# HGRN scores in 32-wide column tiles: small levels as gathered 32x32 blocks, large levels without masks

## The chip, the cores and the metric

The kernel runs on one core of a Trainium2 chip. The metric is device time in microseconds (us) of one execution, the median of several runs; lower is better. A core has TensorE (in the profile PE for matmuls and PEld for the loads of their weights), VectorE (DVE), ScalarE (ACT), GpSimd (POOL) and SyncE (SP, which here issues the weight DMAs).

## The reference

Four post-norm residual layers over 256 tokens of width 1024, each with a token mixer and a SwiGLU feed-forward part. Layers 0 and 3 mix with HGRN2, layer 1 with mLSTM, layer 2 with S5. Only HGRN matters here, with 8 heads of 128 channels:

```python
    log_f = jnp.logaddexp(jnp.log(lb), jnp.log1p(-lb) + jax.nn.log_sigmoid(f))
    k = (1.0 - lb) * jax.nn.sigmoid(-f)
    q = jax.nn.silu(q.astype(jnp.float32))
...
        b = jnp.cumsum(lfb, axis=2)
        diff = b[:, :, :, None, :] - b[:, :, None, :, :]
        decay = jnp.exp(jnp.where(mask[:, :, None], diff, -jnp.inf))
        att = jnp.einsum('bhtd,bhsd,bhtsd->bhts', qb, kb, decay)
        o = jnp.einsum('bhts,bhse->bhte', att, vb) + jnp.einsum('bhtd,bhde->bhte', qb * jnp.exp(b), s_prev)
```

A score of query t and key s is a sum over channels of q times k times the product of the forget gates between s and t, channel by channel. The decay depends on the channel, so it cannot be taken out of the product of q and k.

## The kernel before, in words

All matmuls on weights split their operands into two parts of type F32R (`hi` and `lo`) and take three matmuls (`mm3`, L140 to L142; a wide form at L170 and L173). The weights come in by DMA on SP's queue in 1 MB pieces; ACT copies `hi` (L123), DVE subtracts to get `lo` (L124). A planner keeps the pieces one ahead of their use. The order of instructions on each engine is set when the kernel is built; every engine then works through its list in order, and waits on semaphores.

`hgrn` works on pairs of heads, four pairs to a layer. `hgrn_scores` takes a pair with q and k as tiles of 128 channels by 512 columns: four parts of 128 tokens, in the order (half 0, head 0), (half 0, head 1), (half 1, head 0), (half 1, head 1). It builds the 128x128 score matrices `att` of the four parts, keys in the rows (partitions) and queries in the columns, in a tree. The diagonal comes first: one matmul for each part (L583), multiplied by the identity on DVE (L584). Then, for block sizes m = 1, 2, 4, ... 64, keys of one block of m tokens meet queries of its sibling block: the upper one of each 2m tokens in the first half of the tokens, the lower one in the second half, which is held in reverse.

At a level, ACT gathers the keys side by side into `kk` (L592, 128x256), two matmuls of 128x128 give all their scores with the queries (L594), and DVE's COPY_PREDICATED with a mask from `msk` (L598) puts the wanted ones into `att`. At m = 64 two ACT copies (L609) do this in place of the mask. DVE then multiplies the gate products into k and q for the next level and joins neighbouring products (all through `mul`, L572). A last pair of matmuls (L616) gives the scores between the two halves. `scores` runs two pairs side by side, level by level, and places other work of the layer between the levels: projections of the next queries, of v and of the gate, and `heads_out`, which multiplies the scores with v (L489, L491).

These matmuls read F32 as it is, without a split. Each F32 matmul stands in the trace as two PE records with a weight load each; below, one record is called a pass.

The S5 layer has two other kinds of matmuls that use part of TensorE's columns and that the prediction reads: L1002 and L1004 write 32 partitions from 32 columns of weights, always the same 32; L1090 writes partitions 0 to 63 and 64 to 127 in turn from 64 columns of weights:

```python
                    for f in range(4):
                        for x in range(3):
                            for e in range(2):
                                outputs(py[64 * e : 64 * e + 64, col(f)], b - 1 + e, f, x)
```

Of the kernel before, what the change touches and what calls it, by code (L numbers as in the profile page):

```python
# [9 lines left out]
F32 = mybir.dt.float32  # L10
# [4 lines left out]
ALU = mybir.AluOpType  # L15
AX = mybir.AxisListType

P = 128
# [9 lines left out]
HEAD_EPS = 1e-6  # L28
MASKED = (1, 2, 4, 8, 16, 32)
BIG = 1e30  # L30
# [4 lines left out]
class Trunk:  # L35
# [395 lines left out]
    def hgrn(self, j, gb, lb=None):  # L431

        nc, tc = self.nc, self.tc
        nw = self.const.tile([P, 1], F32, name=f"hnw{j}")
        nc.gpsimd.dma_start(nw, self.a["hg_nw"][j])
        with tc.tile_pool(name=self.uid("hg"), bufs=1, reuse_waits="tile") as hp, \
                tc.tile_pool(name=self.uid("hw"), bufs=2, reuse_waits="tile") as wp:
            msk = hp.tile([P, len(MASKED), 256], F32, name=self.uid("msk"))
            nc.gpsimd.dma_start(msk, self.a["c_lvl"])
# [66 lines left out]
            mem, q, pre, on = {}, {}, {}, {}  # L506
# [9 lines left out]
            def scores(prs, fill):  # L516

                runs = [self.hgrn_scores(wp, q[pr], *pre[pr], msk) for pr in prs]
                for todo in fill:
                    for pr, run in zip(prs, runs):  # L520
                        mem[pr] = next(run)
                    for f in todo:
                        f()
# [39 lines left out]

    def hgrn_scores(self, wp, q, k, f, msk):

# [5 lines left out]
        nc = self.nc  # L571
        mul = lambda o, x, y: nc.vector.tensor_tensor(o, x, y, ALU.mult)  # L572
# [5 lines left out]
        four = lambda x: x.rearrange("p (a t) -> p a t", a=4)  # L578
        att = wp.tile([P, 512], F32, tag="att", name=self.uid("att"), bufs=3)
        k4, q4, a4 = four(k), four(q), four(att)  # L580
        pd = self.bank("a")
        for i in range(4):
            nc.tensor.matmul(pd[:, i * P : (i + 1) * P], k4[:, i], q4[:, i], start=True, stop=True)  # L583
        nc.vector.tensor_tensor(a4, four(pd), self.ident[:, None, :].broadcast_to([P, 4, P]), ALU.mult)  # L584
        mul(q, q, f)
        e, ends = f, wp.tile([P, 256], F32, tag="ends", name=self.uid("ends"))
        spare = 0
        for m in (1, 2, 4, 8, 16, 32, 64):
            n = P // (2 * m)
            pl = self.bank("a")[:, 0:256]  # L590
            kk = wp.tile([P, 2 * P], F32, tag="kk", name=self.uid("kk"))
            nc.scalar.copy(view(kk, 0, (m, 2), (2 * m, 2 * n), (1, m)), keys(k, m))  # L592
            for i in range(2):
                nc.tensor.matmul(pl.rearrange("p (h a t) -> p a h t", h=2, a=2)[:, i], kk[:, i * P : (i + 1) * P],  # L594
                                 view(q, i * P + m, (256 - m, 2), (2 * m, n), (1, m)), start=True, stop=True)
            if m < 64:
                three = lambda x: x.rearrange("p (h b m) -> p h b m", h=2, m=m)
                nc.vector.copy_predicated(queries(att, m), three(i32(msk[:, MASKED.index(m)])), three(pl))  # L598
                for x, s in ((keys(k, m), 1), (queries(q, m), 0)):
                    mul(x, x, whose(e, m, s))  # L600
                new = ends[:, 0 : 4 * n]
# [4 lines left out]
            else:  # L606
                for h in range(2):
                    s = slice(h * m, (h + 1) * m)
                    nc.scalar.copy(a4[s, 2 * h : 2 * h + 2, m - h * m : P - h * m], pl[s, h * P : (h + 1) * P].rearrange("p (a t) -> p a t", a=2))  # L609
                for x, h in ((k4, 0), (q4, 2)):  # L610
# [660 lines left out]
def consts():  # L1271
    s, c = np.arange(P)[:, None], np.arange(64)[None, :]
    lvl = []
    for m in MASKED:
        t = (c // m) * 2 * m + c % m
        same = s // (2 * m) == t // (2 * m)
        lvl.append(np.concatenate([same & ((s // m) % 2 == h) for h in (0, 0, 1, 1)], 1))
    t = np.arange(P)[None, :]
    return {
# [63 lines left out]
```

## Time and profile before

| | |
|---|---|
| median of 3 runs | 1296.07 us (1295.36 to 1298.86) |
| profiled execution, its own time | 1296.3 us |
| its span | 1294.4 us |
| granted TensorE clock | 0.997 |
| busy share of the span | PE 98%, PEld 83%, DVE 75%, ACT 55%, POOL 4% |
| share of PE in the chain that ended last | 89% |
| passes of the scores that the change touches | L583 x64, L594 x224 |

A group row of the profile names the line, the engine, the operation, what it writes and reads, its shapes and its count; then the busy time of the group in us and the mean time of one in ns; then the idle time of the engine just before them and what ended it. In `128*32 128x48` the first part is the weights' size on TensorE (128 rows, 32 columns), the second the result's moving columns. A timeline row has the start in us, the length in us, engine, line and how many instructions it joins; successive PE records overlap, since one takes longer than the distance to the next.

### The profile page before, as it was taken

The numbers are of one execution on the slowest core, as the hardware profiler recorded it, in microseconds if no ns is written. First come the engines' busy times: TensorE is split into PE (matmuls) and PEld (weight loads), VectorE is DVE, ScalarE is ACT, GpSimd is POOL, SyncE is SP. The second block draws the span as 40 slices with busy tenths as digits, with TensorE's granted clock in tenths as the row PEclk, the third lists the DMA queues.
The fourth block names the chain that finished last, engine by engine and source line by source line (L and its number), as shares of the span: only waits on it lengthen the run. The fifth ranks groups of instructions, "written<-read, shape, count | busy, mean of one in ns | idle before, by whom it ended". The sixth has DMA issues, their size and how long they took to land.

```text
span 1294.4 us, 18807 instructions
## 1 busy us (share of the span) xinstructions
PE 1273.3 (98%) x7206; PEld 1073.3 (83%) x7206; DVE 964.8 (75%) x1664; ACT 710.5 (55%) x1134; POOL 53.8 (4%) x77
## 2 busy tenths in 40 slices
PE   8999999999999999999999999999999999999997
PEld 6987788888788888888878778888879878888885
DVE  5888789786688699768489887666595896766664
ACT  5755475665457555657442456555459544555550
POOL 0000200000100110000010000000010001000001
PEclk9999999999999999999999999999999999999999
DMA  8832376757374257756558737555555323755540
GB/s 313 298 131 100 126 247 213 253 179 261 123 260 163 98 202 254 241 199 230 193 219 292 269 131 260 195 184 180 190 208 187 134 97 116 265 190 192 181 149 32
DMA packets 46313, 251.00 MB, mean 194 GB/s; under 512 B 5344, under 2 KB 9456, under 8 KB 19856
## 3 DMA queue, kind: packets, MB, share of 16 engines
q1 hardware_dynamic: 45712, 248.08, 54.0%
q0 software_dynamic: 512, 1.73, 0.4%
q8 instruction: 56, 0.92, 0.3%
q14 instruction: 33, 0.27, 0.1%
HBM read 236.16 MB, written 13.63 MB: 193 GB/s over the span
## 4 chain that ended last, share of the span: by engine, by line
PE 89%; DVE 5%; ACT 2%; issue 1%; DMA 1%; POOL 1%; SPq 0%; POOLq 0%; DVEq 0%; ACTq 0%
PE g L170 18%; PE g L173 9%; PE g L140 9%; PE g L141 9%; PE g L142 9%; PE a L141 8%; PE a L140 8%; PE a L142 8%; PE a L594 2%; DVE lo L124 1%; PE t L225 1%; PE t L1090 1%; PE g L1078 1%; DMA xt<-in_xt 1%; PE t L987 1%
## 5 line engine op out<-in xcount | busy, mean ns | idle before, releaser
L124 DVE TENSOR_TENSOR lo<-w,hi 128x1024 fp32r<-128x1024 f32 (+1 forms) x394 | 476.4, 1217 | 139.5 <-ACT hi L123 128.2
L123 ACT CAST hi<-w 128x1024 fp32r<-128x1024 f32 (+1 forms) x394 | 411.1, 1049 | 194.3 <-PE a L141 109.8
L170 PE MATMUL g<-xx,hi 128*128 128x512 f32 x1024 | 358.5, 395 | 0.0
L173 PE MATMUL g<-xx,lo 128*128 128x256 f32 x1024 | 267.4, 281 | 0.0
L170 PEld LDWEIGHTS g<-xx,hi 128*128 128x128 f32 x1024 | 186.7, 188 | 34.4 <-DVE sum L305 0.3
L173 PEld LDWEIGHTS g<-xx,lo 128*128 128x128 f32 x1024 | 192.5, 188 | 10.4
L140 PE MATMUL g<-hi,xx 128*128 128x512 f32 x416 | 169.5, 408 | 4.6 <-ACT xx L244 2.8
L141 PE MATMUL g<-hi,xx 128*128 128x512 f32 x416 | 166.8, 401 | 0.6 <-DVE xx L1216 0.6
L142 PE MATMUL g<-lo,xx 128*128 128x512 f32 x416 | 166.3, 402 | 0.0
L141 PE MATMUL a<-hi,hl 128*128 128x512 f32 x344 | 135.8, 395 | 0.0
L140 PE MATMUL a<-hi,hh 128*128 128x512 f32 x344 | 135.5, 396 | 0.0
L142 PE MATMUL a<-lo,hh 128*128 128x512 f32 x344 | 135.4, 394 | 0.0
L304 ACT COPY sum<-g 128x256 f32<-128x256 f32 x128 | 47.7, 373 | 147.4 <-PE g L170 147.1
L305 DVE TENSOR_TENSOR sum<-g,sum 128x256 f32<-128x256 f32 x128 | 54.2, 424 | 72.9 <-ACT sum L304 72.6
L140 PEld LDWEIGHTS g<-hi,xx 128*128 128x128 f32 x416 | 78.9, 190 | 23.2 <-ACT xx L244 4.6
L142 PEld LDWEIGHTS g<-lo,xx 128*128 128x128 f32 x416 | 78.7, 189 | 17.4 <-DVE lo L124 1.1
L141 PEld LDWEIGHTS g<-hi,xx 128*128 128x128 f32 x416 | 79.1, 190 | 16.1 <-DVE xx L1216 1.0
L141 PEld LDWEIGHTS a<-hi,hl 128*128 128x128 f32 x344 | 64.7, 188 | 14.9 <-DVE hl L294 0.5
L142 PEld LDWEIGHTS a<-lo,hh 128*128 128x128 f32 x344 | 64.7, 188 | 14.8
L140 PEld LDWEIGHTS a<-hi,hh 128*128 128x128 f32 x344 | 64.3, 188 | 13.7 <-ACT hh L293 0.6
L140 PE MATMUL g<-xx,hi 128*128 128x256 f32 x200 | 56.5, 283 | 0.0
L141 PE MATMUL g<-xx,lo 128*128 128x256 f32 x200 | 56.4, 282 | 0.0
(301 smaller groups left out, 1847.8 us busy)
## 6 DMA issues: line engine op xcount, KB each, us to landing
w<-in_w_gu SPq DMA_DIRECT2D x88, 1024.0 KB, 5.0
w<-in_w_dn SPq DMA_DIRECT2D x44, 1024.0 KB, 5.0
w<-in_w_hg SPq DMA_DIRECT2D x30, 1024.0 KB, 5.1
w<-in_w_ml SPq DMA_DIRECT2D x12, 1024.0 KB, 5.1
gb<-in_ln SPq DMA_DIRECT2D x8, 1024.0 KB, 4.8
w<-in_w_ho SPq DMA_DIRECT2D x8, 1024.0 KB, 4.9
w<-in_w_so SPq DMA_DIRECT2D x8, 1024.0 KB, 7.2
ct<-s5ct SPq DMA_DIRECT2D x8, 768.0 KB, 8.4
```

The lines of the kernel that those rows point to most:

```text
L123: nc.scalar.copy(hi[:, c], part[:, c])
L124: nc.vector.tensor_tensor(lo[:, c], part[:, c], hi[:, c].bitcast(F32), ALU.subtract)
L140: mm(ps, lh, rh, start=start, stop=False)
L141: mm(ps, ll, rh, start=False, stop=False)
L142: mm(ps, lh, rl, start=False, stop=stop)
L170: whole = lambda: mm(ps, hi[:, c], self.xx[:, k].rearrange("p i t -> p (i t)"), start=k == 0, stop=k == KD - 1)
L173: mm(ps[:, S:], lo[:, c], self.xh[:, k], start=False, stop=False)
L225: nc.tensor.transpose(pt[:, (k % 4) * P : (k % 4 + 1) * P], z[:, k * P : (k + 1) * P], self.ident)
L304: nc.scalar.copy(t, ps[:, S:])
L305: nc.vector.tensor_tensor(t, ps[:, 0:S], t, ALU.add)
L594: nc.tensor.matmul(pl.rearrange("p (h a t) -> p a h t", h=2, a=2)[:, i], kk[:, i * P : (i + 1) * P], view(q, i * P + m, (256 - m, 2), (2 * ...
L987: nc.tensor.transpose(ps[:, x * P : (x + 1) * P], k["bz"][:, i, 4 * e + x].rearrange("p j g c -> p (j g c)"), self.ident)
```

## The change

`att` becomes three fixed tiles for each layer, filled with zeros once by POOL. The blocks on the diagonal and the levels m = 1 to 16 are computed as 32x32 blocks only: four matmuls of 32 key columns for each part or gathered half, each to its own 32 partitions of the result, which are four column tiles of TensorE. All of them lie side by side in a tile `near` of 128x128 (four parts of 32 columns), so the mask and the COPY_PREDICATED are a quarter as wide (64 columns in place of 256), and the diagonal's product too (128 in place of 512). Before m = 32 DVE copies `near` into the blocks on `att`'s diagonal with four copies. The levels m = 32 and 64 read q and k in place (no `kk`), in column tiles again, and ACT copies their results straight to `att`, four copies and two. The mask tile shrinks from 128x1536 to 128x384 values: five masks and the pattern of the diagonal.

```diff
-MASKED = (1, 2, 4, 8, 16, 32)
+MASKED = (1, 2, 4, 8, 16)
...
-            msk = hp.tile([P, len(MASKED), 256], F32, name=self.uid("msk"))
+            msk = hp.tile([P, len(MASKED) + 1, 64], F32, name=self.uid("msk"))
+            atts = [hp.tile([P, 512], F32, name=self.uid("att")) for _ in range(3)]
+            for t in atts:
+                nc.gpsimd.memset(t, 0.0)
             nc.gpsimd.dma_start(msk, self.a["c_lvl"])
...
-        att = wp.tile([P, 512], F32, tag="att", name=self.uid("att"), bufs=3)
+        heads = lambda x: x.rearrange("p (a t) -> p a t", a=2)
+        rows = lambda c: slice(32 * c, 32 * c + 32)
+        near = wp.tile([P, P], F32, tag="near", name=self.uid("near"))
         k4, q4, a4 = four(k), four(q), four(att)
-        pd = self.bank("a")
+        pd = self.bank("a")[:, 0:P]
         for i in range(4):
-            nc.tensor.matmul(pd[:, i * P : (i + 1) * P], k4[:, i], q4[:, i], start=True, stop=True)
-        nc.vector.tensor_tensor(a4, four(pd), self.ident[:, None, :].broadcast_to([P, 4, P]), ALU.mult)
+            for c in range(4):
+                nc.tensor.matmul(pd[rows(c), rows(i)], k4[:, i, rows(c)], q4[:, i, rows(c)], start=True, stop=True)
+        nc.vector.tensor_tensor(four(near), four(pd), msk[:, len(MASKED), None, 0:32].broadcast_to([P, 4, 32]), ALU.mult)
...
-            pl = self.bank("a")[:, 0:256]
-            kk = wp.tile([P, 2 * P], F32, tag="kk", name=self.uid("kk"))
-            nc.scalar.copy(view(kk, 0, (m, 2), (2 * m, 2 * n), (1, m)), keys(k, m))
-            for i in range(2):
-                nc.tensor.matmul(pl.rearrange("p (h a t) -> p a h t", h=2, a=2)[:, i], kk[:, i * P : (i + 1) * P],
-                                 view(q, i * P + m, (256 - m, 2), (2 * m, n), (1, m)), start=True, stop=True)
+            pl = self.bank("a")
+            if m < 32:
+                kk = wp.tile([P, 2 * P], F32, tag="kk", name=self.uid("kk"))
+                nc.scalar.copy(view(kk, 0, (m, 2), (2 * m, 2 * n), (1, m)), keys(k, m))
+                pl = pl[:, 0:64]
+                for i in range(2):
+                    for c in range(4):
+                        nc.tensor.matmul(pl[rows(c)].rearrange("p (h a t) -> p a h t", h=2, a=2)[:, i], kk[:, i * P + 32 * c : i * P + 32 * c + 32],
+                                         view(q, i * P + 32 * c + m, (256 - m, 2), (2 * m, 16 // m), (1, m)), start=True, stop=True)
+                three = lambda x: x.rearrange("p (h b m) -> p h b m", h=2, m=m)
+                nc.vector.copy_predicated(view(near, m, (64 - m, 2), (2 * m, 32 // m), (1, m)), three(i32(msk[:, MASKED.index(m)])), three(pl))
+            else:
+                for i in range(2):
+                    for c in range(4):
+                        h = c * 32 // m % 2
+                        t = 32 * c // (2 * m) * 2 * m + m * (1 - h)
+                        nc.tensor.matmul(pl[rows(c), i * m : (i + 1) * m], k4[:, 2 * h + i, rows(c)], q4[:, 2 * h + i, t : t + m], start=True, stop=True)
+                if m == 32:
+                    for c in range(4):
+                        nc.vector.tensor_copy(a4[rows(c), :, rows(c)], four(near[rows(c)]))
+                for s in range(0, P, m):
+                    h = s // m % 2
+                    t = s + m * (1 - 2 * h)
+                    nc.scalar.copy(a4[s : s + m, 2 * h : 2 * h + 2, t : t + m], heads(pl[s : s + m, 0 : 2 * m]))
             if m < 64:
-                three = lambda x: x.rearrange("p (h b m) -> p h b m", h=2, m=m)
-                nc.vector.copy_predicated(queries(att, m), three(i32(msk[:, MASKED.index(m)])), three(pl))
...
             else:
-                for h in range(2):
-                    s = slice(h * m, (h + 1) * m)
-                    nc.scalar.copy(a4[s, 2 * h : 2 * h + 2, m - h * m : P - h * m], pl[s, h * P : (h + 1) * P].rearrange("p (a t) -> p a t", a=2))
```

The change also moves where the groups of score matmuls stand among the projections. Three places show it; a trailing x2 or x8 joins matmuls of one line that follow each other. The first is PE's list in layer 0 at the levels m = 1 and 2 of the first two pairs (`q_548` and `q_609` before, `q_554` and `q_615` after), among the projections of v into `g`. Before:

```order
L142 MATMUL g_841<-lo_769,xx 128x512
L140 MATMUL g_841<-hi_768,xx 128x512
L594 MATMUL a_638<-q_609,kk_639 128x2x64 x2
L594 MATMUL a_647<-q_548,kk_648 128x2x64 x2
L141 MATMUL g_841<-hi_768,xx 128x512
L142 MATMUL g_841<-lo_769,xx 128x512
L140 MATMUL g_842<-hi_768,xx 128x512
L594 MATMUL a_656<-q_609,kk_657 128x2x64 x2
L140 MATMUL a_675<-xx,hi_552 128x2x128
```

And after:

```order
L140 MATMUL g_931<-hi_846,xx 128x512
L141 MATMUL g_931<-hi_846,xx 128x512
L605 MATMUL a_674<-q_615,kk_675 32x2x16 x8
L605 MATMUL a_689<-q_554,kk_690 32x2x16 x8
L142 MATMUL g_931<-lo_847,xx 128x512
L140 MATMUL g_931<-hi_846,xx 128x512
L141 MATMUL g_931<-hi_846,xx 128x512
L605 MATMUL a_704<-q_615,kk_705 32x2x16 x8
L140 MATMUL a_729<-xx,hi_558 128x2x128
```

The groups stand where they stood, among the same neighbours; each has eight small matmuls where it had two of full width.

The second is PE's list at the last two levels, m = 32 and 64, of the same pairs. Before:

```order
L594 MATMUL a_865<-q_548,kk_866 128x2x64 x2
L141 MATMUL g_841<-hi_845,xx 128x512
L594 MATMUL a_874<-q_609,kk_875 128x2x64 x2
L142 MATMUL g_841<-lo_846,xx 128x512
L140 MATMUL g_842<-hi_845,xx 128x512
L141 MATMUL g_842<-hi_845,xx 128x512
L594 MATMUL a_895<-q_548,kk_896 128x2x64 x2
```

And after:

```order
L614 MATMUL a_955<-q_554,k_277 32x32 x8
L140 MATMUL g_931<-hi_935,xx 128x512
L614 MATMUL a_975<-q_615,k_346 32x32 x8
L141 MATMUL g_931<-hi_935,xx 128x512
L142 MATMUL g_931<-lo_936,xx 128x512
L140 MATMUL g_931<-hi_935,xx 128x512
L141 MATMUL g_931<-hi_935,xx 128x512
L614 MATMUL a_1007<-q_554,k_277 32x64 x8
```

Single groups alternate with single projection matmuls, before and after; the weights of the scores are now slices of `k` itself. Over the whole list the score groups that follow each other without another matmul between them form 53 stretches before (L583 and L594) and 48 after (L591, L605 and L614), 24 in each layer.

The third is DVE's list around m = 16 and 32 of these pairs. Before:

```order
L598 COPY_PREDICATED att_611<-msk_132,a_823 128x2x8x16
L572 TENSOR_TENSOR q_548<-q_548,f_272 128x2x8x16
L598 COPY_PREDICATED att_629<-msk_132,a_832 128x2x8x16
L572 TENSOR_TENSOR q_609<-q_609,f_341 128x2x8x16
L572 TENSOR_TENSOR k_271<-k_271,f_272 128x2x4x32
L598 COPY_PREDICATED att_611<-msk_132,a_865 128x2x4x32
L572 TENSOR_TENSOR q_548<-q_548,f_272 128x2x4x32
L598 COPY_PREDICATED att_629<-msk_132,a_874 128x2x4x32
```

And after:

```order
L608 COPY_PREDICATED near_617<-msk_132,a_901 128x2x2x16
L577 TENSOR_TENSOR q_554<-q_554,f_278 128x2x8x16
L608 COPY_PREDICATED near_653<-msk_132,a_916 128x2x2x16
L577 TENSOR_TENSOR q_615<-q_615,f_347 128x2x8x16
L617 COPY att_133<-near_617 32x4x32 x4
L577 TENSOR_TENSOR k_277<-k_277,f_278 128x2x4x32
L577 TENSOR_TENSOR q_554<-q_554,f_278 128x2x4x32
L617 COPY att_134<-near_653 32x4x32 x4
```

The masked copies shrink, the one of m = 32 gives way to four copies out of `near`, and at m = 32 the product into k now comes after the matmul that reads k. On POOL three memsets stand ahead of the DMA of the mask in each layer; in layer 3 these lie between the two reciprocal roots (L182, L183) of the layernorm that ends layer 2. SP's list is unchanged.

More of the change, by code (lines that the diff above doesn't have):

```diff
@@ L516, in scores @@
             def scores(prs, fill):
-                runs = [self.hgrn_scores(wp, q[pr], *pre[pr], msk) for pr in prs]
+                runs = [self.hgrn_scores(wp, q[pr], *pre[pr], msk, atts[pr % 3]) for pr in prs]
                 for todo in fill:
@@ L562, in hgrn_gates, with hgrn_scores @@
         return k, f
-    def hgrn_scores(self, wp, q, k, f, msk):
+    def hgrn_scores(self, wp, q, k, f, msk, att):
         nc = self.nc
@@ L596, in hgrn_scores @@
             if m < 64:
-                three = lambda x: x.rearrange("p (h b m) -> p h b m", h=2, m=m)
-                nc.vector.copy_predicated(queries(att, m), three(i32(msk[:, MASKED.index(m)])), three(pl))
-                for x, s in ((keys(k, m), 1), (queries(q, m), 0)):
-                    mul(x, x, whose(e, m, s))
+                for x, y in ((keys(k, m), 1), (queries(q, m), 0)):
+                    mul(x, x, whose(e, m, y))
                 new = ends[:, 0 : 4 * n]
@@ L1271, in consts @@
 def consts():
-    s, c = np.arange(P)[:, None], np.arange(64)[None, :]
+    s, c = np.arange(P)[:, None], np.arange(16)[None, :]
     lvl = []
@@ L1275, in consts @@
         t = (c // m) * 2 * m + c % m
-        same = s // (2 * m) == t // (2 * m)
+        same = s % 32 // (2 * m) == t // (2 * m)
         lvl.append(np.concatenate([same & ((s // m) % 2 == h) for h in (0, 0, 1, 1)], 1))
+    lvl.append(s % 32 == np.arange(64)[None, :])
     t = np.arange(P)[None, :]
```

## Prediction

> **What bounds the kernel now.** I read the page first: its busy times, then the groups of the lines that change, then the stages in windows, and last the timeline at the places where matmuls of few columns begin and end.
>
> ```profile
> span 1294.4 us, 18807 instructions
> PE 1273.3 (98%) x7206; PEld 1073.3 (83%) x7206; DVE 964.8 (75%) x1664; ACT 710.5 (55%) x1134; POOL 53.8 (4%) x77
> PE 89%; DVE 5%; ACT 2%; issue 1%; DMA 1%; POOL 1%; SPq 0%; POOLq 0%; DVEq 0%; ACTq 0%
> ```
>
> TensorE bounds the whole: it has 89% of the chain that ended last. Whatever moves the end here must be PE time, or time in which PE waits. The stages of the scores are next, layer 0 in the first two windows and layer 3 in the last two (length, then busy time of each engine):
>
> ```profile
> 56.00:88.00 32.00, 31.85 (x224) 28.32 (x223) 27.73 (x64) 16.81 (x32) 0.00 (x0) 1.00 0.40 143
> 88.00:122.00 34.00, 32.62 (x189) 26.94 (x188) 29.39 (x67) 16.42 (x31) 1.86 (x2) 1.00 0.25 86
> 1002.00:1034.00 32.00, 31.70 (x222) 28.16 (x221) 28.85 (x65) 18.47 (x35) 0.00 (x0) 1.00 0.37 132
> 1034.00:1069.00 35.00, 33.66 (x194) 27.72 (x193) 29.47 (x67) 17.12 (x33) 1.84 (x2) 1.00 0.32 114
> ```
>
> Added up, PE is busy 129.8 of 133 us and DVE 115.4, 87%: DVE is the second bound, and ACT (68.8) is none. The lines that the change touches:
>
> ```profile
> L594 PE MATMUL a<-q,kk 128*128 128x128 f32 x224 | 35.5, 285 | 3.1 <-DVE q L572 2.4 <-ACT kk L592 0.3
> L594 PEld LDWEIGHTS a<-q,kk 128*128 128x128 f32 x224 | 29.8, 189 | 13.7 <-issue 5.4 <-ACT kk L592 5.2 <-DVE q L572 1.2
> L583 PE MATMUL a<-q,k 128*128 128x128 f32 x64 | 8.5, 276 | 0.1
> L598 DVE COPY_PREDICATED att<-msk,a 128x256 f32<-128x256 int32 x48 | 25.6, 534 | 2.9 <-PE a L594 2.7
> L584 DVE TENSOR_TENSOR att<-a,ident 128x512 f32<-128x512 f32 x8 | 5.5, 686 | 5.1 <-PE a L583 5.1
> L592 ACT COPY kk<-k 128x256 f32<-128x256 f32 x56 | 22.6, 411 | 21.6 <-DVE k L572 13.1 <-PE a L594 7.3 <-DVE f L572 0.7
> L609 ACT COPY att<-a 64x128 f32<-64x128 f32 x16 | 4.1, 259 | 3.3 <-PE a L594 1.9 <-DVE q L572 1.2
> ```
>
> The passes overlap in the records, so their cost is the distance of their starts, not their length. The timeline of one stretch of the diagonal gives it, and shows what its edges cost:
>
> ```profile
> 55.87 0.28 PE L141 MATMUL a<-xx,lo 128*128 128x256 f32 x1
> 55.99 0.29 PE L142 MATMUL a<-xx,hi 128*128 128x256 f32 x1
> 56.12 1.05 PE L583 MATMUL a<-q,k 128*128 128x128 f32 x8
> 56.93 0.48 PE L140 MATMUL g<-hi,xx 128*128 128x512 f32 x1
> 57.24 0.39 PE L141 MATMUL g<-hi,xx 128*128 128x512 f32 x1
> ```
>
> Eight passes in 1.05 us, each 0.276 long: (1.05 - 0.276) / 7 = 0.111 us a pass. The entry costs nothing (0.13 after L142, where 0.12 is usual). The last pass began at 56.12 + 1.05 - 0.276 = 56.89; L141 follows at 57.24, 0.35 later, which is one pass and one projection matmul (0.23, below). So the edges are free now.
>
> **The change, term by term.** *Removed on PE:* 224 + 64 = 288 passes x 0.111 = 32.0 us.
>
> *Added on PE:* per pair 16 matmuls for the diagonal, 8 at each of seven levels, 72 in all; two passes each, eight pairs: 1152 passes. Their price hangs on whether the four column tiles work at once. The S5 layer has the nearest rows, all of 32 columns on the same 32 partitions, and two tiles of 64 columns in turn:
>
> ```profile
> L1002 PE MATMUL t<-bc,big 128*32 128x16 f32 x128 | 9.0, 183 | 0.0
> L1004 PE MATMUL t<-t,big 128*32 128x48 f32 x128 | 9.8, 207 | 0.0
> L1090 PE MATMUL t<-ct,s5hs 128*64 128x128 f32 x128 | 11.5, 276 | 1.3 <-DVE s5hs L1131 1.3
> ```
>
> ```profile
> 271.07 0.39 PE L141 MATMUL a<-hi,hl 128*128 128x512 f32 x1
> 271.30 0.40 PE L142 MATMUL a<-lo,hh 128*128 128x512 f32 x1
> 271.63 0.30 PE L1002 MATMUL t<-bc,big 128*32 128x16 f32 x4
> ...
> 272.54 0.28 PE L1002 MATMUL t<-bc,big 128*32 128x16 f32 x4
> 272.66 0.34 PE L1004 MATMUL t<-t,big 128*32 128x48 f32 x4
> 272.93 0.50 PE L170 MATMUL g<-xx,hi 128*128 128x512 f32 x1
> 273.27 0.40 PE L173 MATMUL g<-xx,lo 128*128 128x256 f32 x2
> ...
> 692.77 0.61 PE L1090 MATMUL t<-ct,s5hs 128*64 128x128 f32 x8
> 693.21 0.39 PE L1090 MATMUL t<-ct,s5u 128*64 128x128 f32 x4
> 693.43 0.61 PE L1090 MATMUL t<-ct,s5hs 128*64 128x128 f32 x8
> ```
>
> On one tile a pass of 16 moving columns takes (0.28 - 0.183) / 3 = 0.032 us, one of 48 takes (0.34 - 0.207) / 3 = 0.044. A column more lengthens a pass by (276 - 183) / 112 = 0.83 ns; 48 columns make 0.040 of the 0.044, but 16 would make 0.013, so something else, the load of 32 columns of weights, sets the 0.032. With 32 moving columns (0.027) I take 0.032, with 64 (level 64) 0.054.
>
> L1090 tells of tiles at once: from 692.77 to 693.43 it makes 12 passes in 0.66 us, 0.055 each, though 128 moving columns alone take 128 x 0.83 = 0.106. The two tiles overlap fully, loads included. If four do as well, a pair costs (8 passes a tile for the diagonal + 6 levels x 4) x 0.032 + 4 x 0.054 = 1.24 us, and eight pairs 9.9 us. If only two do: 19.8. If none: 39.7. I take four, since nothing in L1090's rows shows a loss at two; four at once, and F32 columns so short, are shown nowhere, so both other values stay for the range.
>
> A rule speaks against the overlap. The Trainium skill, "TensorE: Matmul & The Clock Gate", section "The mechanism" (of packing), says that a weight load overlaps running matmuls only when its row group differs; column tiles share all rows. By it a tile would pay load and stream in turn, an estimate of 0.032 + 0.027 a pass here, and the added passes would take 17.9 us in place of 9.9. The trace disagrees: of L1090's 0.055 a pass half a stream is 0.053, which leaves no room for a load.
>
> *Edges.* Going from a 512-wide projection matmul into a stretch of column tiles takes 271.63 - 271.30 = 0.33 in place of 0.23 (271.30 - 271.07), and the first four passes 0.30 in place of 0.28: 0.12 us. Coming out, the last pass of L1004 starts at 272.66 + 0.34 - 0.207 = 272.79; L170 comes 0.14 later in place of 0.044, and L173 follows it after 0.34 in place of 0.23: 0.20 us. An edge pair is 0.32 us, and the order has 48 stretches: 48 x 0.32 = 15.4 us. This eats half of what the passes give; one group of 16 passes costs 4 x 0.032 + 0.32 = 0.45 us, just the 4 x 0.111 = 0.44 that it cost before. Only the 20 stretches that hold a diagonal or two groups gain. Where PE waits anyway, the entry is hidden.
>
> PE's own sum: 9.9 + 15.4 - 32.0 = -6.7 us.
>
> *DVE.* The small sizes have these rows, which are ordinary products:
>
> ```profile
> L572 DVE TENSOR_TENSOR k<-k,f 128x256 f32<-128x256 f32 x40 | 16.5, 416 | 0.0
> L572 DVE TENSOR_TENSOR f<-ends 128x128 f32<-128x128 f32 x8 | 2.3, 286 | 0.0
> L572 DVE TENSOR_TENSOR f<-f 128x64 f32<-128x64 f32 x8 | 1.7, 214 | 0.0
> L1007 DVE TENSOR_TENSOR dg<-ident,s5dd 32x128 f32<-32x128 f32 x8 | 2.2, 278 | 0.2
> ```
>
> A pair gives up 0.686 + 6 x 0.534 = 3.89 us and takes 0.286 (diagonal) + 5 x 0.27 (0.214, raised by the 534 to 416 that a masked copy takes over a product of 256) + 4 x 0.278 = 2.75. Eight pairs: -9.1 us of 115.4. It reaches the end only through PE's waits. Those before the level matmuls are at most the 13.7 us of L594's weight loads, which have some length of their own. The gain lies between 0 and 8 us; I take 3, near the lower end: DVE stays at 106 of some 124 us, as dense as before, and what falls away is chiefly an entry edge hidden in a wait.
>
> *ACT.* Two gathers of 411 ns go, four copies of 32 partitions come (259 ns is the nearest row, of twice the data): 0 to +0.2 us a pair, on an engine half idle. Hidden by PE's stretches; without that cover 1.7 us.
>
> *New waits.* At m = 32 and 64 PE reads k itself, so DVE's product into k (row `k_277` above) waits for PE; before, it waited for the gather. Behind it stand q's product, which waited for PE before too, and the `lo` splits, for which the projections wait. Cost: one product's time, 0.42, for each of eight pairs at worst, 3.4 us; I take 0, since q's product stood there. *Fixed `att` tiles:* pair 3 reuses pair 0's, as the rotation of three did.
>
> *POOL.* Three memsets of 128x512 in each layer:
>
> ```profile
> 155.86 0.53 POOL L935 MEMSET tm<- 128x512 f32 x1
> 949.13 0.63 POOL L439 DMA_DIRECT2D msk<-in_c_lvl  x1 [2.66 <-PE t L288]
> 957.16 1.04 POOL L182 TENSOR_SCALAR rs<-mv 128x1 f32<-128x1 f32 x1 [7.40 <-DVE mv L208]
> ```
>
> 1.6 us, after a wait on TensorE like that of the mask's DMA, and 7.4 us of idle time before the root behind them: 0, at worst 0.5 if they wait for the last matmul of layer 2. The mask's smaller DMA is not waited for: 0. SP's queue is unchanged.
>
> Together: -6.7 - 3 = -9.7 us. The profiled execution took 1296.3 us (span 1294.4), 0.2 over the median; against the median 1296.1 - 9.7 = 1286.4.
>
> **The rivals.** *One tile at a time (slower).* Small passes follow each other at 0.032 us whatever the tile, as L1002's do: 39.7 + 15.4 - 32.0 - 3 = +20.1, 1316 us. It decides from (32.0 - 15.4 + 3) / 1152 = 0.017 us a pass. For it: no row here has passes closer than 0.032 on average. Against: L1090. The Trainium skill, "TensorEngine Tiling (Array Packing)", section "Instruction Overhead", says that each matmul has about 60 cycles of overhead and that a tiling factor should not be taken from a dimension that is small already; 16 and 32 columns are. At the 2.4 GHz that the same notes give TensorE, that is an estimate of 0.025 us a pass, and the kernel would take 1305; no row here shows such a floor across tiles.
>
> *Two tiles at a time.* 19.8 + 15.4 - 32.0 - 3 = +0.2, 1296: the edges take all. For it: two is all that a row shows.
>
> *PE's gain becomes a wait.* DVE, 100% busy in parts of the stage, keeps its pace; PE's 6.7 us come back as waits: 1294 to 1296.
>
> *The edges cost little.* If PE waits at most stretches, their entries (0.12) vanish, and DVE's gain counts fully: -6.7 - 8 = -15, 1281.
>
> **How the numbers follow.** Four tiles at once with edges paid: 0.50, 1282 to 1291. Two at a time, or a shallow overlap: 0.20, 1291 to 1299. One at a time, wholly or in part (0.020 to 0.032 a pass): 0.18, 1300 to 1316. The gain turned into waits: 0.08. Edges hidden: 0.04, 1278 to 1282. The range 1279 to 1304 leaves out most of the third case, 0.14, and the low end of the last, 0.01. A measurement of this kernel tells 0.3% (3.9 us) from no change: faster are the first and last case and a sixth of the second, 0.57; the same are most of the waits and half of the second, 0.17; slower the third and the rest, 0.26.
>
> **What would show it.** In the profile after, the groups L605 and L614 should show their passes, by fours, some 0.035 us apart, a group of 16 in 0.15 to 0.2; after a stretch the next projection matmul should be 0.2 late. L608 should mean about 270 ns, DVE in the stages 9 us less. If 16 passes spread over 0.4 us or more, the overlap fails and the kernel is slower; if they take 0.15 and the time still stands, the waits before L605 will have grown.

## The result, and the profile after

The changed kernel took 1285.82 us, the median of 4 runs (1283.62 to 1288.83), against 1296.43 us (1295.36 to 1298.86) for the kernel before beside it. The ratio is 0.9921, with a 95% interval from 0.9906 to 0.9936: by it the change takes 10.2 us less (8.3 to 12.2). The prediction was 1286.4 us, 9.7 less. The profiled execution took 1287.31 us, 1.5 over its median.

The page of the kernel after: its span, the busy times, and the engines' shares of the chain that ended last.

```profile
span 1285.5 us, 20596 instructions
PE 1263.6 (98%) x8070; PEld 1056.3 (82%) x8070; DVE 955.1 (74%) x1688; ACT 710.1 (55%) x1150; POOL 57.2 (4%) x83
PE 91%; DVE 3%; ACT 2%; DMA 1%; issue 1%; POOL 1%; SPq 0%; POOLq 0%; DVEq 0%; ACTq 0%
```

PE was busy 9.7 us less than before (1273.3) and the span is 8.9 us shorter, so the time came out of what the profile counts as PE's work and not out of its idle time, which is 21.9 us now and was 21.1. DVE has 9.7 us less work (964.8 before); 9.1 was expected. TensorE still bounds the whole.

The groups of the new lines after, each shape by itself: four of those that replace L583 and L594 on PE (L614 has as many passes of 32 columns again), then the masked copy and the copies out of `near`.

```profile
L605 PE MATMUL a<-q,kk 128*32 128x32 f32 x640 | 11.7, 200 | 2.4 <-DVE near L608 2.4
L605 PEld LDWEIGHTS a<-q,kk 128*32 128x32 f32 x640 | 8.2, 110 | 12.5 <-issue 8.1 <-ACT kk L601 2.9 <-DVE q L577 0.7
L591 PE MATMUL a<-q,k 128*32 128x32 f32 x256 | 3.8, 198 | 0.1
L614 PE MATMUL a<-q,k 128*32 128x64 f32 x128 | 3.0, 223 | 0.2
L608 DVE COPY_PREDICATED near<-msk,a 128x64 f32<-128x64 int32 x40 | 10.2, 256 | 4.4 <-PE a L605 3.6
L617 DVE COPY att<-near 32x128 f32<-32x128 f32 x32 | 6.9, 216 | 0.4
```

L608 means 256 ns where 270 were forecast, and L617 216 where 278 were. The idle time of PE before the levels is as it was: 2.4 us before L605's matmuls, 3.1 before L594's. The wait on which the prediction kept an eye did not grow.

The timeline of PE after, in layer 0: a stretch of two groups of one level with the projection matmuls around it, and one group of m = 64.

```profile
60.68 0.40 PE L140 MATMUL g<-hi,xx 128*128 128x512 f32 x1
60.91 0.40 PE L141 MATMUL g<-hi,xx 128*128 128x512 f32 x1
61.24 0.46 PE L605 MATMUL a<-q,kk 128*32 128x32 f32 x32
61.63 0.50 PE L142 MATMUL g<-lo,xx 128*128 128x512 f32 x1
61.97 0.39 PE L140 MATMUL g<-hi,xx 128*128 128x512 f32 x1
...
81.61 0.43 PE L614 MATMUL a<-q,k 128*32 128x64 f32 x16
```

32 passes take 0.46 us with the last one's 0.200 (L605's mean): (0.46 - 0.200) / 31 = 0.0084 us a pass. On one tile it would be 0.032. At m = 64 it is (0.43 - 0.223) / 15 = 0.014. The edges are there as well. The entry is 61.24 - 60.91 = 0.33 in place of 0.23. The last pass starts at 61.24 + 0.46 - 0.20 = 61.50, and L142 follows 0.13 later; the matmul behind it comes after 0.34 in place of 0.23.

A ruler for single layers is the roots that POOL takes (L182): one follows the mixer of layer 0, one ends layer 2, and the last comes near the end of the kernel. The timeline of POOL, the first and the last of these in the kernel before (the middle one stands in the prediction, at 957.16), then the three of the kernel after:

```profile
144.24 1.07 POOL L182 TENSOR_SCALAR rs<-mv 128x1 f32<-128x1 f32 x1 [7.21 <-DVE mv L208]
1288.00 0.75 POOL L182 TENSOR_SCALAR rs<-mv 128x1 f32<-128x1 f32 x1 [8.91 <-DVE mv L208]
```

```profile
138.89 1.07 POOL L182 TENSOR_SCALAR rs<-mv 128x1 f32<-128x1 f32 x1 [7.21 <-DVE mv L208]
954.15 1.04 POOL L182 TENSOR_SCALAR rs<-mv 128x1 f32<-128x1 f32 x1 [6.41 <-DVE mv L208]
1279.14 0.75 POOL L182 TENSOR_SCALAR rs<-mv 128x1 f32<-128x1 f32 x1 [8.91 <-DVE mv L208]
```

Layer 3 takes 1288.00 - 957.16 = 330.84 us before and 1279.14 - 954.15 = 324.99 after: 5.85 us less, from one profiled execution each. Layer 0's root comes 144.24 - 138.89 = 5.35 us earlier, so the time was won in the two layers where the change was made. Of the 11.2 us of both, 2.3 are lost again between them, where nothing was changed; the windows of PE in layer 2, before and after, show most of it (length, PE busy, granted clock, DMA share, GB/s):

```profile
700.00:706.00 6.00, 6.00 (x36) 1.00 0.80 312
```

```profile
700.00:706.00 6.00, 4.70 (x48) 0.72 0.81 302
```

In the profiled execution of the change the granted clock fell to 0.72 here, 6 x 0.28 = 1.7 us of work not done.

The same ruler parts layer 3 into what PE does and what it waits for. The windows of PE between the two roots, before and after:

```profile
957.16:1288.00 330.84, 326.76 (x1839) 1.00 0.46 161
```

```profile
954.15:1279.14 324.99, 321.20 (x2271) 1.00 0.46 164
```

PE is as full as before: it is busy 5.56 us less and idle 0.29 us less (3.79 in place of 4.08).

### The profile page after: what moved, and what is told of

It is laid out like the page before. It is cut to its first block, busy times and chain, and to the rows that moved or that the text cites. A ratio compares the mean times of both kernels' runs of the same rounds, so it can differ in the third digit from the quotient of the medians.

```text
span 1285.5 us, 20596 instructions
## 1 busy us (share of the span) xinstructions
PE 1263.6 (98%) x8070; PEld 1056.3 (82%) x8070; DVE 955.1 (74%) x1688; ACT 710.1 (55%) x1150; POOL 57.2 (4%) x83
## 4 chain that ended last, share of the span: by engine, by line
PE 91%; DVE 3%; ACT 2%; DMA 1%; issue 1%; POOL 1%; SPq 0%; POOLq 0%; DVEq 0%; ACTq 0%
PE g L170 18%; PE g L173 9%; PE g L140 9%; PE g L142 9%; PE g L141 9%; PE a L141 9%; PE a L140 8%; PE a L142 8%; PE t L1111 1%; PE g L1099 1%; DVE lo L124 1%; PE t L225 1%; DMA w<-in_w_gu 1%; DMA xt<-in_xt 1%; PE a L605 1%
## 5 line engine op out<-in xcount | busy, mean ns | idle before, releaser
L173 PEld LDWEIGHTS g<-xx,lo 128*128 128x128 f32 x1024 | 192.4, 188 | 10.5
L142 PE MATMUL g<-lo,xx 128*128 128x512 f32 x416 | 167.0, 403 | 0.0
L142 PE MATMUL a<-lo,hh 128*128 128x512 f32 x344 | 135.4, 393 | 0.0
L142 PEld LDWEIGHTS g<-lo,xx 128*128 128x128 f32 x416 | 78.7, 189 | 18.3 <-DVE lo L124 1.3
L142 PEld LDWEIGHTS a<-lo,hh 128*128 128x128 f32 x344 | 64.7, 188 | 14.8
```

Source lines behind the costliest of these rows:

```text
L142: mm(ps, lh, rl, start=False, stop=stop)
L173: mm(ps[:, S:], lo[:, c], self.xh[:, k], start=False, stop=False)
```

## The experiments

The theory to test has three parts: four column tiles work at once; each stretch of them costs PE some 0.3 us at its edges; DVE's smaller masks give little. The rivals: the gain is DVE's; the tiles overlap less; the edges are free. All results in one table: the ratio to the kernel before with its interval, the difference worked out from it (times 1296.1 us), and layer 3 between the two roots, against 330.84 us, from one profiled execution.

| run | what it is | ratio, 95% | us against before | layer 3 |
|---|---|---|---|---|
| after | the change | 0.9921 (0.9906 to 0.9936) | -10.2 | -5.85 |
| e1_dve_only | DVE's part alone | 0.9994 (0.9985 to 1.0003) | -0.8 | -0.54 |
| e2_pe_only | column tiles alone | 0.9943 (0.9930 to 0.9955) | -7.4 | -3.63 |
| e3_one_tile | all on one tile | 1.0071 (1.0057 to 1.0085) | +9.2 | +4.65 |
| e4_two_tiles | all on two tiles | 0.9968 (0.9956 to 0.9981) | -4.1 | -2.61 |
| e5_more_edges | 37 more stretches | 1.0002 (0.9993 to 1.0011) | +0.3 | -0.19 |
| f5_together | two pairs' groups joined | 0.9881 (0.9866 to 0.9896) | -15.4 | -7.86 |
| f7_before_together | the same in the kernel before | 0.9988 (0.9979 to 0.9997) | -1.6 | -0.80 |
| f6_four | four pairs' groups joined | 0.9884 (0.9867 to 0.9901) | -15.0 | -7.85 |
| f8_tail | f6 with another end | 0.9940 (0.9927 to 0.9953) | -7.8 | -2.97 |

### The two halves apart

*DVE's part alone:* the small tiles and masks of the change, with score matmuls of full width as before. In short:

```diff
-            for c in range(4):
-                nc.tensor.matmul(pd[rows(c), rows(i)], k4[:, i, rows(c)], q4[:, i, rows(c)], start=True, stop=True)
+            nc.tensor.matmul(pd[:, i * P : (i + 1) * P], k4[:, i], q4[:, i], start=True, stop=True)
...
+                    nc.tensor.matmul(pw.rearrange("p (h a t) -> p a h t", h=2, a=2)[:, i], kk[:, i * P : (i + 1) * P],
+                                     view(q, i * P + m, (256 - m, 2), (2 * m, n), (1, m)), start=True, stop=True)
...
```

> The narrow work of VectorE alone: the score matmuls are again two of 128x128 for a level and four for the diagonal, as before the change, and VectorE and ScalarE take only the first 64 (or 32) of their columns, as after it, so the scores are not the reference's. Theory: TensorE's gain of 6.7 us is missing and VectorE's 9 us of shorter work shorten waits by about 3 us: 1293 us, between 1290 and 1296. Rival one, the whole gain comes from VectorE: 1286. Rival two, VectorE's work is hidden: 1296.

It took 1294.42 us: 0.8 us less than before, and the interval (1.9 less to 0.4 more) takes in no change. That is nearer the second rival than the 3 us of the theory. The page's busy times of this run:

```profile
PE 1271.5 (98%) x7206; PEld 1073.4 (83%) x7206; DVE 955.3 (74%) x1688; ACT 711.5 (55%) x1150; POOL 57.0 (4%) x83
```

DVE lost 9.5 us of work, as in the change, and the end moved by less than a tenth of that.

*The column tiles alone:* the matmuls of the change, with DVE's operations stretched again to 256 and 512 columns.

```diff
-                nc.vector.copy_predicated(view(near, m, (64 - m, 2), (2 * m, 32 // m), (1, m)), three(i32(msk[:, MASKED.index(m)])), three(pl))
+                nc.vector.copy_predicated(four(near)[:, :, 0:64], i32(msk[:, MASKED.index(m)])[:, None, :].broadcast_to([P, 4, 64]), pl[:, None, :].broadcast_to([P, 4, 64]))
...
                 if m == 32:
-                    for c in range(4):
-                        nc.vector.tensor_copy(a4[rows(c), :, rows(c)], four(near[rows(c)]))
+                    nc.vector.copy_predicated(four(near)[:, :, 0:64], i32(msk[:, 0])[:, None, :].broadcast_to([P, 4, 64]), pl[:, None, 0:64].broadcast_to([P, 4, 64]))
```

> The column tiles alone: TensorE's matmuls are those of the changed kernel (51 stretches), but VectorE works at the old width: 512 columns for the diagonal, 256 at each masked copy including one for m = 32, by reading the narrow result four times over; the blocks are not brought to their places, so the scores are not the reference's. Theory: 9.9 + 51 x 0.32 - 32.0 = -5.8 us of TensorE, no relief of waits: 1290 to 1291 us. Rival one (all from VectorE): 1296. Rival two (all from TensorE): 1286.

It took 1287.4 us, 7.4 us less than before (5.8 to 9.1), nearer the second rival (all from TensorE) than the theory, though DVE kept most of its load (962.7 us in place of 964.8). The group of its masked copy at the first levels:

```profile
L608 DVE COPY_PREDICATED near<-msk,a 128x256 f32<-128x256 int32 x40 | 17.8, 446 | 4.8 <-PE a L605 4.6
```

So most of the gain is PE's. The two halves give -0.8 and -7.4, -8.2 together, where the whole gave -10.2; the intervals are 1.2 to 2 us wide to each side, so they do not tell this from a plain sum. Whether DVE's relief is worth 0.8 us, as alone, or up to 2.8, as the difference of the whole and this run (which has three stretches more), stays open. Layer 3 leans to more than a plain sum: its halves give 0.54 and 3.63 where the whole gave 5.85. The window of PE between the roots of this run says why:

```profile
952.07:1279.28 327.21, 322.10 (x2271) 1.00 0.45 163
```

PE is busy 4.66 us less than before, and idle 5.11 us in place of 4.08: with DVE at its old pace, 1.0 us of PE's gain in layer 3 comes back as waits. With the whole change it is 3.79.

### How many tiles work at once

The same matmuls, with the results for the diagonal and the levels up to m = 32 all put on one column tile, or on two in turn:

```diff
-                nc.tensor.matmul(pd[rows(c), rows(i)], k4[:, i, rows(c)], q4[:, i, rows(c)], start=True, stop=True)
+                nc.tensor.matmul(pd[rows(0), rows(i)], k4[:, i, rows(c)], q4[:, i, rows(c)], start=True, stop=True)
...
```

The levels have the same edit; the version on two tiles has `rows(c % 2)`.

> The changed kernel with all 32-column matmuls of the diagonal and of the levels m = 1 to 32 on one column tile: every one writes partitions 0 to 31, the readers read those, and the rest of the scores is left out, so the output is not the reference's. Count and size of the matmuls are the same, 42 stretches. Theory (four tiles worked at once, passes 0.033 apart on one): a pair has 128 passes at 0.033 in place of 32 such times, +3.2 us, eight pairs +25, less 6 edge pairs: +23 over the changed kernel, 1309 us. Rival, the passes lie beside VectorE's work anyway: half of that or less, under 1298.

> The same with two column tiles in turn (partitions 0 to 31 and 32 to 63), the other half of the scores left out; 46 stretches. Theory: 64 times 0.033 for a pair in place of 32, eight pairs +8.4 us, less 2 edge pairs: +8 over the changed kernel, 1293 to 1294 us. That was the rival of the prediction that put the time at no change. Rival, two tiles suffice because something else sets the pace: under 1288.

They took 1304.49 and 1291.92 us. From the timelines of PE, a stretch of 32 passes of one level on one tile, and on two:

```profile
60.29 1.20 PE L605 MATMUL a<-q,kk 128*32 128x32 f32 x32
```

```profile
61.17 0.70 PE L605 MATMUL a<-q,kk 128*32 128x32 f32 x32
```

With 0.197 and 0.198 for the last pass, a pass takes 0.0324 us on one tile and 0.0162 on two; on four it was 0.0084. Each doubling halves it: the overlap is complete, loads of weights included, up to all four. On the clock the loss is smaller than 1024 passes give: (0.0324 - 0.0084) x 1024 = 24.6, less 1.9 for 6 stretches fewer, is 22.7 us, and 19.4 were measured against the change (from the ratios, some 2.7 to each side); for two tiles 8.0 - 0.6 = 7.4 against 6.1. In layer 3 the version on one tile takes 4.65 + 5.85 = 10.5 us more than the change, 21.0 for two such layers. PE's idle time there is 3.61 us in place of 3.79, so what is still missing against 22.7 is not hidden in waits.

### What an edge costs

A projection-like matmul of 128x64, whose result nothing reads, between the two halves of each group of the levels up to 16: 85 stretches in place of 48.

```diff
-                pl = pl[:, 0:64]
+                spill, pl = pl[:, 256:320], pl[:, 0:64]
                 for i in range(2):
+                    if i:
+                        nc.tensor.matmul(spill, self.xh[:, 0, 0:P], self.xh[:, 0, 0:64], start=True, stop=True)
                     for c in range(4):
```

> The changed kernel with one full-width matmul of 64 columns put in the middle of each of the 40 groups of the levels m = 1 to 16; its result is not used. 85 stretches in place of 48. Theory: 37 more edge pairs at 0.32 us and 40 streams of 0.03: +13 us, 1299. Rival, the edges lie in waits that are there anyway: +4 or less, under 1290.

The whole gain was gone: 1296.27 us, a ratio of 1.0002, where the theory had 1299. The timeline of PE around one added matmul (L605 in this kernel; the groups are its L607):

```profile
58.32 0.27 PE L607 MATMUL a<-q,kk 128*32 128x32 f32 x8
58.52 0.30 PE L605 MATMUL a<-xx 128*128 128x64 f32 x1
58.74 0.28 PE L607 MATMUL a<-q,kk 128*32 128x32 f32 x8
```

The last pass of the first eight starts at 58.32 + 0.27 - 0.205 = 58.385, the next pass of the level at 58.74: 0.355 us in place of 0.009. 64 columns at 0.83 ns are 0.05 of it, so leaving and entering cost 0.30 on the spot. On the clock it is 10.5 us for 40 matmuls, 0.26 each with the matmul itself (0.20 to 0.32), where the spot gives 0.35. Part of the rest lies in waits: between the roots of layer 3 PE is idle 3.05 us (330.65 less 327.60 busy) in place of 3.79. So edges are not free, and one costs PE 0.30 us where it does not wait anyway.

### Fewer edges

If edges cost that much, joining them pays. In this version the two pairs that run side by side write their scores of one level to one bank, and PE's order is set so that the groups of both stand together: 34 stretches in place of 48. In short (`met` holds what the pairs share):

```diff
-                    for pr, run in zip(prs, runs):
-                        mem[pr] = next(run)
+                    while True:
+                        outs = [next(run) for run in runs]
+                        if outs[0] == "mm":
+                            outs = [next(run) for run in runs[::-1]][::-1]
+                        if outs[0]:
+                            break
+                    mem.update(zip(prs, outs))
...
-            pl = self.bank("a")
+            if ("p", m) not in met:
+                met["p", m] = self.bank("a")
+                pl = met["p", m][:, 0:w]
+            else:
+                pl = met["p", m][:, w : 2 * w]
...
+                        for x in met[m] if ("mm", m) not in met else met["mm", m]:
+                            self.tc.add_manual_dep(mm, x.name, dep, reason="pairs together")
```

> The changed kernel with the two pairs of a step in lockstep: both pairs' matmuls of a level follow each other, the later pair's first, into one PSUM bank, so that 34 stretches are left of 48; all the rest of the computation is the same. Theory: 14 edge pairs less at 0.32 us: -4.5, 1281 us. Rival, the earlier pair now waits for the later one and the wait costs as much as the edges: 1285 or more.

It took 1279.42 us, by the ratios 5.2 less than the change (some 2.7 to each side), where the theory had 4.5. Its page's busy times, and the diagonals of two pairs on its timeline of PE:

```profile
PE 1255.4 (98%) x8070; PEld 1053.4 (82%) x8070; DVE 954.4 (75%) x1688; ACT 710.2 (56%) x1150; POOL 57.3 (4%) x83
```

```profile
83.72 0.40 PE L142 MATMUL g<-lo,xx 128*128 128x512 f32 x1
84.05 0.76 PE L601 MATMUL a<-q,k 128*32 128x32 f32 x64
84.75 0.50 PE L140 MATMUL g<-hi,xx 128*128 128x512 f32 x1
```

The 64 passes stand between one entry (0.33 after L142) and one exit, 0.70 us from the first pass to the next projection matmul. PE is busy 8.2 us less than after the change with the same passes. Of that 3.5 us are not the order's: in the first 30 us the granted clock was 1.00 in this profiled execution and 0.94 in that of the change (1.8 us), and it kept 1.00 in the window 700 to 706 (1.7 us). That leaves 4.7 us, or 0.34 for each of 14 stretches. Layer 3, free of both, is 2.0 us shorter (7.86 against 5.85), 0.25 for each of the 8 stretches that it saves.

Is it the edges, or does the new order help any kernel? The same order in the kernel before, whose matmuls of full width have edges that the prediction read as free:

> The kernel before, full-width matmuls and wide masks, with the two pairs in lockstep as in f5_together: both pairs' matmuls of a level follow each other, the later pair's first, into one bank. Full-width stretches have free edges. Theory (f5_together gained by its fewer edges): no change from before, 1295 to 1297. Rival, the lockstep itself shortens waits and would have done so without column tiles: 1293 or less.

1294.39 us, 1.6 less than before (0.4 to 2.7), between the theory and the rival. But the gain is not in waits: PE's idle time is 21.6 us in place of 21.1, and its busy time is 2.4 us less (1270.9), for 21 stretches fewer (32 in place of 53), 0.11 each. So a saved stretch is worth something in the kernel before too, about a third of what it is worth with column tiles. The edges of full width are not quite free; the part on the prediction comes back to this.

Then all four pairs of a layer at once, 16 stretches. All four queries now come ahead of the scores, and `heads_out(0)`, which stood between the groups of the last two pairs, behind them:

```diff
-            query(0)
-            query(1)
+            for pr in range(4):
+                query(pr)
...
-            scores((0, 1), ([], [lambda: query(2)], [], [lambda: query(3)], v1[0:1], v1[1:2], v1[2:3], v1[3:]))
-            scores((2, 3), ([lambda: heads_out(0)], g0[0:1], g0[1:2], g0[2:3], g0[3:], g1[0:1], g1[1:2], g1[2:3]))
+            scores((0, 1, 2, 3), ([], v1[0:2], v1[2:], g0[0:2], g0[2:], g1[0:1], g1[1:2], g1[2:3]))
+            heads_out(0)
```

> All four pairs of a layer go through the levels together, and the groups of one level stand together in PE's list: 16 stretches in place of 34 in the version with two pairs together (48 in the change as given). Theory (the edges cost about 0.3 us a pair wherever PE is the bound): 18 edge pairs fewer are 18 x 0.3 = 5.4 us less than the 1279.4 of two pairs together, about 1274. Rival (DVE and ACT bind, since four pairs have to finish a level before PE can go on, and only the projections of v and of the gate are there to fill the time): PE waits before each group, and the time is 1279 or more.

1279.56 us, as with two pairs. The busy times of its page, then the wait that is new in its list of waits (engine, line, released by: us in all, times, longest):

```profile
PE 1251.3 (98%) x8070; PEld 1053.1 (82%) x8070; DVE 954.3 (75%) x1688; ACT 710.7 (56%) x1150; POOL 57.8 (5%) x85
```

```profile
PE t L398 <- DVE on L506: 4.9, 4, 1.5
```

PE's work did fall, by 4.1 us or 0.23 for each of 18 stretches; four waits, 4.9 us together, took its place. The rival's time was right and its place wrong: the waits are not before the groups but behind them, where the transposes of `head_turn` (L398) wait for DVE to norm and gate the heads, with no projection left to fill the time.

The last run tried to fill it: one more piece of the gate's projection kept back, and the second `heads_out` moved ahead of the last piece.

```diff
-            scores((0, 1, 2, 3), ([], v1[0:2], v1[2:], g0[0:2], g0[2:], g1[0:1], g1[1:2], g1[2:3]))
+            scores((0, 1, 2, 3), ([], v1[0:2], v1[2:], g0[0:2], g0[2:], g1[0:1], g1[1:2], []))
             heads_out(0)
             gb = gb()
+            g1[2]()
+            heads_out(1)
             g1[3]()
             for h in range(2):
                 turn(0, h)
-            heads_out(1)
```

> The version with four pairs together, with its end arranged anew: the products with v of the second half of the heads come before the last piece of the gate's projection, and one piece more is kept back for this place. Theory (four pairs together did save their edges, 1255.4 - 1251.3 = 4.1 us of PE's busy time, and lost them to the four waits of 4.9 us for the normed heads behind the scores): those waits go, one of up to 1 us a layer may come before the products with v, which now follow the last scores at once, and the time is 1275 to 1277. Rival (DVE's chain of the norm, multiplication and split is itself the bound there, or PE waits for the copies of the last scores as long): 1279 to 1280 as without it.

1288.11 us: it lost 8.6 us by the medians, 7.2 by the ratios, and the times of both the theory and its rival were wrong; the rival's cause, DVE's chain as the bound at this place, is what the profile shows. Its waits of PE, and its windows of PE at the end of the scores in layers 0 and 3 (length, PE busy, granted clock, DMA share, GB/s):

```profile
PE g L141 <- DVE ol L248: 5.9, 2, 3.0
PE g L140 <- ACT oh L247: 3.2, 2, 1.9
```

```profile
120.00:124.00 4.00, 0.96 (x3) 0.90 0.00 0
124.00:128.00 4.00, 4.00 (x13) 0.67 0.44 102
...
1060.00:1064.00 4.00, 1.45 (x4) 0.73 0.00 0
1064.00:1069.00 5.00, 3.79 (x10) 0.53 0.13 31
```

The waits at L398 are gone, but the split of the turned heads (`oh`, `ol`) now comes last with nothing behind it: 9.1 us in place of 4.9. The other half of the loss is the clock: in the windows behind these pauses TensorE was granted 0.67 of it for 4 us in layer 0 and 0.53 for 5 us in layer 3, which is 4 x 0.33 + 5 x 0.47 = some 3.7 us of work not done, the 1.2 us that PE still waits in the second included. 4.2 and 3.7 make 7.9, about the whole loss. The timeline of PE behind the second pause:

```profile
1065.21 0.80 PE L141 MATMUL g<-hi,ol 128*128 128x512 f32 x1 [2.90 <-DVE ol L248]
1065.80 0.63 PE L142 MATMUL g<-lo,oh 128*128 128x512 f32 x1
1066.23 0.63 PE L140 MATMUL g<-hi,oh 128*128 128x512 f32 x1
```

Matmuls of 512 columns follow each other by 0.43 us in place of 0.23. No version came out below the one with two pairs together, 1279.42 us.

## Why the prediction was right, and where it was not

**Four tiles at once: right, and shown.** The forecast was 0.032 / 4 = 0.008 us a pass and 0.0135 at m = 64; the trace has 0.0084 and 0.014. The added passes come to 1024 x 0.0084 + 128 x 0.014 = 10.4 us where 9.9 were forecast. The runs on one and on two tiles show that a smaller overlap gives the times of the first two rivals in their order: slower than before, and between before and after. That the load of 32 columns sets the 0.032 of one tile, as the prediction has it, no run tells apart from another floor of a tile.

The rule of the Trainium skill that a weight load overlaps running matmuls only with another row group ("TensorE: Matmul & The Clock Gate", section "The mechanism") would have given 17.9 / 1152 = 0.016 a pass; the trace disagrees, with loads of 110 ns and a pass every 8.4. The Trainium skill's overhead of some 60 cycles for each matmul ("TensorEngine Tiling (Array Packing)", section "Instruction Overhead") is 0.025 us by the prediction's estimate. Across tiles the trace disagrees with it too, with 0.0084; for one tile, at 0.032, no run here tests it.

**Edges of the column tiles: right.** On the spot a pair costs what was forecast: 0.10 at the entry, 0.12 and 0.11 behind it, 0.33 in all. The added part of the sum, 9.9 + 15.4 = 25.3 us, can be measured as a whole: over all stretches of the trace after, the time from the start of the matmul ahead of a stretch to the start of the second one behind it, less the usual steps of the projections (0.23 us for 512 columns, 0.12 for 256) and less PE's idle time, comes to some 26.5 us, an estimate from the starts of the records. On the clock 0.26 (0.20 to 0.32) was measured for an inserted matmul and its pair, and 0.23 to 0.34 for joined stretches; part of an edge can lie where PE waits, as the sum said of the entry.

**The removed term: too small.** PE's own sum was -6.7 us, and in layer 3 alone PE is busy 5.56 us less. Added up in the same way, the stretches of the kernel before take some 37.8 us, where the sum had 32.0; 26.5 - 37.8 is -11.3, and twice 5.56 is 11.1. The 0.111 us a pass and the free edges were read from one stretch of eight. Of 53 stretches 38 have four passes, and in 25 of these the second pass starts 0.14 to 0.22 us after the first, in place of 0.111. Two of one kind on the timeline of PE before, and the weight load of the first:

```profile
1010.71 0.40 PE L141 MATMUL g<-hi,xx 128*128 128x512 f32 x1
1011.15 0.70 PE L594 MATMUL a<-q,kk 128*128 128x128 f32 x4
1011.59 0.37 PE L140 MATMUL a<-xx,hi 128*128 128x256 f32 x1
1011.80 0.27 PE L141 MATMUL a<-xx,lo 128*128 128x256 f32 x1
...
1020.09 0.39 PE L140 MATMUL g<-hi,xx 128*128 128x512 f32 x1
1020.32 0.61 PE L594 MATMUL a<-q,kk 128*128 128x128 f32 x4
1020.68 0.36 PE L140 MATMUL a<-xx,hi 128*128 128x256 f32 x1
1020.88 0.28 PE L141 MATMUL a<-xx,lo 128*128 128x256 f32 x1
```

```profile
1011.12 0.41 PEld L594 LDWEIGHTS a<-q,kk 128*128 128x128 f32 x3 [0.45 <-ACT kk L592]
```

From the 512-wide matmul to the second one behind, the late stretch takes 1.09 us and the other 0.79, which is what 0.23 + 4 x 0.111 + 0.12 gives. The first waited for its keys. PE counts as busy meanwhile, since the record of the matmul ahead is 0.40 us long where the next one could start after 0.23. So time went away with the old stretches that neither the price of a pass nor PE's idle time showed. The run with the two pairs joined in the kernel before won part of it. The share of such waits in the 5.8 us between 37.8 and 32.0 was not worked out. DVE's relief is not needed for it: with the column tiles alone PE is already busy 4.66 us less in layer 3.

**DVE: 3 us was a choice within bounds; as shorter waits of PE it did not come.** In layer 3 PE's idle time fell by 0.29 us, 0.6 for two such layers, and over the whole profile it did not shrink. Alone the relief gave 0.8 us (at most 1.9), on top of the column tiles 2.8, with an interval that reaches the smaller figure. What it does there is to keep PE's gain from coming back as waits: without it PE is idle 5.11 us in layer 3. That was a case of its own in the prediction, with a chance of 0.08, and the run with column tiles alone shows a little of it.

**So the total was right with two errors against each other:** PE's part came out larger by 4 to 5 us than forecast, and the waits that DVE's relief was to shorten hardly shrank. That 9.7 comes so near to 10.2 is in this measure luck; the mechanism, four tiles at once with edges paid, is not.

**New waits, POOL, ACT: right at nothing.** PE waited 2.4 us in all for DVE before L605 in the profile after; ACT is busy 710.1 us in place of 710.5. The roots of POOL, behind the new memsets in its queue, were not late (the idle time before the second root that ends layer 2 fell from 7.40 to 6.41 us).

## What to carry to other kernels

Small F32 matmuls of 32 columns in four column tiles ran four times as fast as on one tile, but each change between them and full-width matmuls costs some 0.3 us of TensorE time where it does not wait anyway: lay many side by side, and count the stretches in PE's order before the passes. Joining the groups of two chains, which gained 1.6 us before, was worth a third to a half of the change itself once the edges had a higher price. Read the price of what goes away from many places and not from one: a busy TensorE can hide late starts. When TensorE is the bound, work taken from a half-hidden engine shows up only as far as TensorE waits for it, and the filling taken away from one wait is missed at the next.

## What the runs showed of the hardware

A pass of 32 rows of the result and 32 moving columns takes 32.4 ns on one tile, 16.2 on two and 8.4 on four, so the issue of matmuls is no limit down to 8.4 ns here.

In the last run the granted clock fell at pauses of PE, of 1.3 and 3.0 us in layer 0 and of 1.9 and 2.9 us in layer 3. In layer 3 it was at half before the second pause began, as the window of the last matmuls ahead of that pause shows (length, PE busy, granted clock, DMA share, GB/s):

```profile
1061.90:1062.30 0.40, 0.40 (x2) 0.50 0.00 0
```

The slow clock cost some 3.7 us beside the 9.1 of waiting. In the version with four pairs, whose waits were of up to 1.5 us, the window over the same place kept its clock:

```profile
1034.00:1069.00 35.00, 31.26 (x233) 1.00 0.41 151
```

But a pause that short is not safe: in the profile of the change the clock of 0.72 between 700 and 706 us came with a single wait of 1.30 us in the S5 layer, and the kernel before, with a wait of 1.29 us at the same matmul, kept 1.00. So the length of a pause alone does not tell, in these runs, whether the clock falls.

The Trainium skill, "TensorE: Matmul & The Clock Gate", section "What's actually happening", says that TensorE falls to half its clock after an idle window of about 3.4 us and comes back after as long a busy one. The spacing of 0.43 in place of 0.23 agrees with about half; none of these pauses was as long as that window, so of the idle window no run here shows the rule as it stands.

In the first 30 us the granted clock differed from execution to execution, 0.94 in the profile of the change and 1.00 in that of the version with two pairs together. Layer 3 by itself is free of that.
